# An FFN's right operands summed by adding DMAs, and its last chunk by seven products

## The chip, the core and the metric

The kernel runs on one core of a Trainium2 chip. The metric is the device time of one execution in microseconds (us); before the change it is 1135.33 us, the median of 3 runs (1135.29 to 1135.79). The five engines are TensorE (PE, with its weight loads PEld), VectorE (DVE), ScalarE (ACT), GpSimd (POOL) and SyncE (SP), which issues the DMAs of the kernel before.

## The reference

Two layers over x of 512 tokens by 1024 columns, in float32. Layer 0 mixes tokens by latent attention, layer 1 by an mLSTM; each is followed by the same feed-forward network, the part that matters here, with 4096 hidden columns:

```python
def sqrelu_mlp(h, w1, w2):
    return jnp.square(jax.nn.relu(h @ w1)) @ w2

def reference(x, norm_mix, norm_ffn, ...):
    for i in range(DEPTH):
        hn = rms_norm(x, norm_mix[i])
        ...
        x = x + y.astype(x.dtype)
        x = x + sqrelu_mlp(rms_norm(x, norm_ffn[i]), ffn_w1[i], ffn_w2[i]).astype(x.dtype)
    return x
```

## The kernel before

The program has four stages in a row: latent attention, FFN 0 (about 244 to 581 us of the span), mLSTM, FFN 1 (about 791 us to the end, 1134). Every product of two float32 matrices is made of three matmuls in fp32r: each operand is split into a high part (a cast, on ACT) and a low part (operand less high part, on DVE). For a weight the parts are called wh and wl (`split_w`, lines 155 to 170), for the hidden activations hh and hl.

One FFN is cut along its 4096 hidden columns into 8 chunks c (`NC`). In a chunk the first product takes four units F, each 24 matmuls of 128x512 that give 128 hidden columns for all 512 tokens. `f_post` (lines 755 to 784) runs relu and square on ACT into a tile z; after every second F, GpSimd forms four sums of quarters of z (S1 to S4), and then both halves of z are split into hh and hl, the first 768 columns one unit later, the other 1024 two units later (list `later`).

The second product of chunks 0 to 6 is not a plain product of 2x2 blocks with eight block products but Winograd's form with seven, called P0 to P6 (`PROD`, lines 737 and 738). Each has a left operand (a quarter of hidden activations or a sum), a right operand (a quarter b11 to b22 of the chunk of w2, or one of the sums t1 to t4), and a chain: products of chain a add up in one pair of PSUM banks, those of b and c in another pair, and after each product its state is read by `y_add` (line 827), which adds it, times the norm's factor r2, into the residual x on DVE, once for each token tile. A product has 12 matmuls. Since the next product on a chain writes the same banks, it has to wait for the `y_add` of the one before. The sums t1 to t4 are made by GpSimd out of the loaded quarters (`s_sum`, lines 792 to 801), in tiles tw (6 of them); SP loads the quarters (`s_load`). The last chunk (c = 7) is plain: `l_mm` (line 839), 8 block products of 12 matmuls. In FFN 1 the result is then transposed on TensorE, copied out of PSUM into one of two tiles t (`out`, lines 851 to 864) and stored, 256 KB a time; in FFN 0 it becomes the input of the mLSTM (`Norm.half`).

TensorE, DVE, ACT and GpSimd run in program order here (class `InOrder`, lines 72 to 80; all such instructions show as L80 in the profile). The order is the list `units` (lines 867 to 874), with a unit's split two units ahead and w1 loads four units ahead (`ahead`, line 877). Before, a chunk runs as P0 F P1 P2 F P3 P4 F P5 F P6, where the F units belong to the next chunk; chunk 6, with three F units left, as P0 F P1 F P2 P3 F P4 P5 P6. Only SP's queue is ordered by the scheduler.

## Time and profile before

| | before |
|---|---|
| median of 3 runs | 1135.33 us |
| profiled execution | 1136.02 us |
| its span, first to last instruction | 1134.0 us |
| TensorE busy | 1111.6 us, 98% |
| DVE busy | 823.3 us, 73% |
| ACT busy | 557.9 us, 49% |
| GpSimd busy | 451.4 us, 40% |
| mean granted TensorE clock | 0.998 |
| DMA | 104.27 MB, 92 GB/s, 30.1% of 16 engines |

The span is what the trace covers; the profiled execution's own time is 2.0 us longer. TensorE is busy nearly all the time, so the reader looks for the few places where it isn't, and for what it waits there. A tile's name stands without its number: tw is a tile of w2 quarters, wr one of w1, x the residual, tp and mm PSUM banks.

### The profile page before, as it was taken

Reading aid. Unit: us, or ns where it says so; the run is one execution under the profiler, and the core shown is the slowest. Engines: PE = TensorE matmul, PEld = TensorE weight load, DVE = VectorE, ACT = ScalarE, POOL = GpSimd, SP = SyncE. Lnnn points to the kernel's source line nnn. Section 1 sums busy time; section 2 is a strip of 40 time slices with the busy share of each in tenths; the row PEclk is TensorE's granted clock in tenths of the full one; section 3 lists DMA queues with packets and bytes.
Section 4 is the critical chain, followed back from the end, with each engine's and each line's share of the span. In section 5 each row is a group of like instructions: output and inputs, shape, how many; then the busy total and the mean of one; then the engine's idle time right before and its main releaser. Section 6 shows DMA issues by size and latency. Waiting matters only on the chain.

```text
span 1134.0 us, 15668 instructions
## 1 busy us (share of the span) xinstructions
PE 1111.6 (98%) x5802; PEld 949.0 (84%) x5802; DVE 823.3 (73%) x1286; ACT 557.9 (49%) x985; POOL 451.4 (40%) x454
## 2 busy tenths in 40 slices
PE   7899999999999999999999999999999999999998
PEld 7889988888888888888898898888888888888886
DVE  7689997456798798788756565554578779779863
ACT  4468876336544444534545344332655444444441
POOL 6667785207356347335010011000537437436500
PEclk9999999999999999999999999999999999999999
DMA  6301021433432432343203223232343343333112
GB/s 202 117 25 47 20 76 38 132 98 124 128 99 74 127 112 84 102 123 89 85 21 100 87 59 91 81 90 86 136 113 91 93 130 93 93 112 111 57 56 75
DMA packets 32428, 104.27 MB, mean 92 GB/s; under 512 B 3424, under 2 KB 6752, under 8 KB 32352
## 3 DMA queue, kind: packets, MB, share of 16 engines
q1 hardware_dynamic: 32352, 103.27, 30.1%
q8 instruction: 46, 0.75, 0.3%
q14 instruction: 30, 0.25, 0.1%
HBM read 101.16 MB, written 2.10 MB: 91 GB/s over the span
## 4 chain that ended last, share of the span: by engine, by line
PE 93%; DVE 3%; POOL 2%; ACT 1%; issue 1%; DMA 0%; SPq 0%; ACTq 0%; POOLq 0%
PE mm L80 39%; PE tp L80 38%; PE mm L178 4%; PE mm L177 4%; PE mm L176 4%; PE po L80 3%; PE tp L178 1%; PE tp L177 1%; PE tp L176 1%; DVE wl L80 1%; ACT t L80 1%; DVE x L80 1%; POOL x L80 0%; DMA x<-in_xT 0%; POOL scr L80 0%
## 5 line engine op out<-in xcount | busy, mean ns | idle before, releaser
L80 PE MATMUL mm<-xg,wh 128*128 128x512 f32 (+1 forms) x1088 | 319.1, 377 | 0.0
L80 POOL TENSOR_TENSOR z<-z 128x256 f32<-128x256 f32 x112 | 129.5, 1175 | 320.2 <-ACT z L80 318.0
L80 PEld LDWEIGHTS mm<-xg,wh 128*128 128x128 f32 x1088 | 200.2, 188 | 37.4
L80 DVE TENSOR_TENSOR wl<-tw,wh 128x1024 fp32r<-128x1024 f32 x100 | 174.5, 1745 | 74.9 <-ACT wh L80 74.9
L80 PE MATMUL mm<-xg,wl 128*128 128x512 f32 (+1 forms) x544 | 206.3, 379 | 0.0
L80 POOL TENSOR_TENSOR tw<-tw,tw 128x1024 f32<-128x1024 f32 x56 | 159.8, 2862 | 34.6 <-issue 29.2
L80 DVE SCALAR_TENSOR_TENSOR x<-tp,r,x 128x512 f32<-128x512 f32 (+1 forms) x215 | 149.8, 733 | 14.2 <-PE tp L80 14.1
L80 PE MATMUL tp<-wh,hl 128*128 128x512 f32 x408 | 159.0, 390 | 0.9 <-DVE hl L80 0.9
L80 DVE TENSOR_TENSOR wl<-wr,wh 128x1024 fp32r<-128x1024 f32 (+1 forms) x72 | 119.6, 1661 | 55.4 <-ACT wh L80 55.4
L80 PE MATMUL tp<-wh,hh 128*128 128x512 f32 x408 | 159.1, 390 | 0.0
L80 PE MATMUL tp<-wl,hh 128*128 128x512 f32 x408 | 158.7, 389 | 0.0
L80 ACT ACTIVATE t<-mm 128x512 f32<-128x512 f32 (+3 forms) x97 | 54.3, 560 | 204.1 <-PE mm L80 195.0
L80 PEld LDWEIGHTS mm<-xg,wl 128*128 128x128 f32 x544 | 102.3, 188 | 22.9 <-DVE wl L80 4.5
L80 ACT CAST wh<-tw 128x1024 fp32r<-128x1024 f32 x100 | 104.7, 1047 | 34.1 <-PE tp L80 26.2
L80 ACT CAST wh<-wr 128x1024 fp32r<-128x1024 f32 (+1 forms) x74 | 78.9, 1067 | 32.1 <-PE tp L80 27.7
L166 DVE TENSOR_TENSOR wl<-wr,wh 128x1024 fp32r<-128x1024 f32 (+2 forms) x43 | 51.2, 1194 | 55.8 <-ACT wh L162 55.6
L80 PEld LDWEIGHTS tp<-wh,hl 128*128 128x128 f32 x408 | 76.6, 188 | 17.7 <-DVE hl L80 1.7
L80 PEld LDWEIGHTS tp<-wh,hh 128*128 128x128 f32 x408 | 76.6, 188 | 16.5 <-ACT zw L80 0.8
L80 PEld LDWEIGHTS tp<-wl,hh 128*128 128x128 f32 x408 | 76.6, 188 | 15.8
L80 ACT CAST hh<-z 128x1024 fp32r<-128x1024 f32 (+1 forms) x60 | 56.9, 949 | 53.0 <-POOL z L80 53.0
L80 DVE TENSOR_TENSOR hl<-z,hh 128x1024 fp32r<-128x1024 f32 (+1 forms) x60 | 80.7, 1345 | 0.0
L162 ACT CAST wh<-wr 128x1024 fp32r<-128x1024 f32 (+2 forms) x43 | 42.8, 995 | 66.7 <-PE mm L177 31.6
(281 smaller groups left out, 2063.7 us busy)
## 6 DMA issues: line engine op xcount, KB each, us to landing
wr<-in_w SPq DMA_DIRECT2D x64, 512.0 KB, 3.6
tw<-in_w SPq DMA_DIRECT2D x64, 512.0 KB, 3.6
wr<-in_w_qkv SPq DMA_DIRECT2D x8, 640.0 KB, 4.1
wr<-in_w_oa SPq DMA_DIRECT2D x8, 512.0 KB, 3.7
wr<-in_w_mo SPq DMA_DIRECT2D x8, 512.0 KB, 3.5
wr<-in_w_ob SPq DMA_DIRECT2D x8, 512.0 KB, 3.6
wr<-in_w_v SPq DMA_DIRECT2D x6, 512.0 KB, 3.9
wr<-in_w_z SPq DMA_DIRECT2D x8, 336.0 KB, 4.9
```

The costliest lines, as they stand in the source:

```text
L80: return lambda *args, **kw: tc.keep_in_program_order(f(*args, **kw)) if self.on else f(*args, **kw)
L162: act.copy(hi[:, :n], raw[:, :n])
L166: dve.tensor_sub(lo[:, :n], raw[:, :n], hi[:, :n].bitcast(F32))
L176: pe.matmul(out, lhsT=lh, rhs=rh, start=start, stop=False)
L177: pe.matmul(out, lhsT=lh, rhs=rl, start=False, stop=False)
L178: pe.matmul(out, lhsT=ll, rhs=rh, start=False, stop=stop)
```

## The change

GpSimd no longer subtracts tw tiles. The left operands' signs are turned so that every right sum is a sum without minus (up to the sign, which goes into r2: `r2[:, 1]` is its negative), and each is made by a DMA on GpSimd's queue that reads a quarter of w2 and adds it to what lies in the tile (`accum_op=add`): t1 = b12 + b11, then in the same tile t2 = t1 + b22 and t4 = t2 + b21, each after the split that reads the sum before; t3 = b22 + b12. A chunk has four such DMAs beside four loads on SP. The high part of the negated sums is made by ACT with scale -1, the low part by a scalar_tensor_tensor on DVE.

The order of the products changes (S2 t2 and S4 b22, and S3 t3 and A12 b21, change places), and the units of chunks 0 to 5 run as P0 P1 F P2 P3 F P4 P5 F P6 F; chunk 6 stays P0 F P1 F P2 P3 F P4 P5 P6.

The last chunk is made by the seven products too: P0, P1, P4, P2, P3, then P5 and P6 cut by token tile with outputs between. Its sums t1 to t3 stand in halves of two z tiles, begun by three loads of b12 and adding DMAs during chunk 6; t4 is one tensor_add on GpSimd. In numbers: 24 matmuls fewer (12 in each FFN), 56 subtractions on GpSimd replaced by 64 adding DMAs and 2 additions.

The diff's core:

```diff
-        PROD = ((A11, "b11", "a", (0, 0)), (S1, "t1", "b", (1, 1)), (S2, "t2", "a", (0, 1)), (S4, "b22", "b", (0, 1)),
-                (S3, "t3", "a", (1, 1)), (A12, "b21", "c", (0, 0)), (A22, "t4", "a", (1, 0)))
+        PROD = ((A11, "b11", "a", (0, 0)), (S1, "t1", "b", (1, 1)), (S4, "b22", "b", (0, 1)), (S2, "t2", "a", (0, 1)),
+                (A12, "b21", "c", (0, 0)), (S3, "t3", "a", (1, 1)), (A22, "t4", "a", (1, 0)))
+        PLACE = {"b11": "b11", "b12": "b12", "b22": "b22", "b21": "b21", "t1": "b12", "t2": "b12", "t4": "b12", "t3": "b22"}
+        ADD = {"t1": "b11", "t2": "b22", "t4": "b21", "t3": "b12"}
...
+                else:
+                    iact.activation(hi[:, b], z[:, b], AF.Copy, scale=-1.0)
+                    idve.scalar_tensor_tensor(lo[:, b], z[:, b], -1.0, hi[:, b].bitcast(F32), op0=mult, op1=sub)
...
+            later.append([s_now[0] + 1, lambda: split(slice(0, 3), 1)])
+            later.append([s_now[0] + (2 if i > 3 else 1), lambda: split(slice(3, 7), -1)])
...
+        def l_load():
+            C = NC - 1
+            for n in ("t1", "t2"), ("t3", "t4"):
+                z = fp.tile([P, 2, D], F32, tag="z", bufs=3, name=nm("z"))
+                for i in range(2):
+                    tw[C, n[i]] = z[:, i]
+                    if n[i] != "t4":
+                        nc.sync.dma_start(z[:, i], a["w2"][layer, C, QUARTER.index("b12")])
+        def l_sum(*todo):
+            for n, b in todo:
+                ipool.dma_start(tw[NC - 1, n], a["w2"][layer, NC - 1, QUARTER.index(b)], accum_op=add)
         def s_sum(c, n):
-            b = lambda n: tw[c, n]
-            if n == "t1":
-                tw[c, n] = fp.tile([P, D], F32, tag="tw", bufs=6, name=nm("tw"))
-                ipool.tensor_sub(b("t1"), b("b12"), b("b11"))
-            else:
-                x, y, to = {"t2": ("b22", "t1", "b11"), "t3": ("b22", "b12", "b12"), "t4": ("b21", "t2", "t1")}[n]
-                ipool.tensor_sub(b(to), b(x), b(y))
+            ipool.dma_start(tw[c, PLACE[n]], a["w2"][layer, c, QUARTER.index(ADD[n])], accum_op=add)
         def s_split(c, n):
...
+            if n in (1, 2, 3) and c < NC - 1:
+                s_sum(c, ("t2", "t3", "t4")[n - 1])
...
-        for c in range(NC - 1):
-            for k in range(7):
+        for c in range(NC):
+            for k in range(7) if c < NC - 1 else (0, 1, 4, 2, 3):
                 units.append(("P", c, k))
-                if k in ((0, 2, 4, 5) if c < NC - 2 else (0, 1, 3)):
+                if n < 4 * NC and k in ((1, 3, 5, 6) if c < NC - 2 else (0, 1, 3)):
...
+        C = NC - 1
+        s_mm(C, 5, (0,))()
+        half(0, (0,))
+        s_mm(C, 5, (1,))()
+        half(0, (2, 4, 6))
+        s_mm(C, 6, (0,))()
+        half(1, (4, 6))
         if last:
-            out(4, (3,))
+            post = s_mm(C, 6, (1,))
+            out(0, (2,))
+            post()
...
+            out(0, (3,))
```

How the rows of an order read: operation, the tile written, the tiles read, the shape, and what it waits for.

DVE, the end of chunk 6 in FFN 1, before. The rows begin at the split of P6's right operand (wl from tw); hl is the hidden activations' low part, x from tp a `y_add`, tp_1849 and tp_1850 the banks of chain a, tp_1859 and tp_1860 those of P5.

```order
L80 TENSOR_TENSOR wl_1882_10343<-tw_1840_10085,wh_1881_10342 128x1024 [waits PE_49,Activation_49]
L80 TENSOR_TENSOR hl_1880_10329<-z_1867_10252,hh_1879_10328 128x1024 [waits Activation_49]
L80 SCALAR_TENSOR_TENSOR x_689_3187<-tp_1849_10144,r2_1506_8032,x_689_3187 128x512 [waits PE_49]
L80 SCALAR_TENSOR_TENSOR x_691_3191<-tp_1850_10145,r2_1506_8032,x_691_3191 128x512 [waits PE_49]
L80 TENSOR_TENSOR wl_1886_10355<-tw_1871_10274,wh_1885_10354 128x1024 [waits DMAHW2_49,Activation_49]
L80 SCALAR_TENSOR_TENSOR x_684_3177<-tp_1859_10199,r2_1506_8032,x_684_3177 128x512 [waits PE_49]
L80 SCALAR_TENSOR_TENSOR x_686_3181<-tp_1860_10200,r2_1506_8032,x_686_3181 128x512 [waits PE_49]
L80 TENSOR_TENSOR zw_1887_10372<-tw_1883_10350,zw_1887_10372 128x1024 [waits DMAHW4_49,Activation_49]
L80 SCALAR_TENSOR_TENSOR x_688_3185<-tp_1849_10144,r2_1506_8032,x_688_3185 128x512 [waits PE_49]
L80 SCALAR_TENSOR_TENSOR x_690_3189<-tp_1850_10145,r2_1506_8032,x_690_3189 128x512 [waits PE_49]
```

The same place now; tp_1841 and tp_1842 are chain a, on which both P5 and P6 run, and tp_1851 and tp_1852 are the banks of P4.

```order
L80 TENSOR_TENSOR wl_1875_10372<-tw_1802_9899,wh_1874_10371 128x1024 [waits DMASW3_49,PE_49,Activation_49]
L80 TENSOR_TENSOR hl_1873_10354<-z_1859_10271,hh_1872_10353 128x768 [waits Activation_49]
L80 SCALAR_TENSOR_TENSOR x_684_3177<-tp_1851_10214,r2_1505_8051,x_684_3177 128x512 [waits PE_49]
L80 SCALAR_TENSOR_TENSOR x_686_3181<-tp_1852_10215,r2_1505_8051,x_686_3181 128x512 [waits PE_49]
L80 TENSOR_TENSOR wl_1879_10396<-tw_1865_10298,wh_1878_10395 128x1024 [waits DMAHW2_49,Activation_49]
L80 SCALAR_TENSOR_TENSOR hl_1873_10354<-z_1859_10271,hh_1872_10353 128x1024 [waits Activation_49]
L80 SCALAR_TENSOR_TENSOR x_689_3187<-tp_1841_10155,r2_1505_8051,x_689_3187 128x512 [waits PE_49]
L80 SCALAR_TENSOR_TENSOR x_691_3191<-tp_1842_10156,r2_1505_8051,x_691_3191 128x512 [waits PE_49]
L80 TENSOR_TENSOR wl_1881_10417<-z_1861_10275,wh_1880_10416 128x1024 [waits DMASW4_49,Activation_49]
L80 SCALAR_TENSOR_TENSOR x_688_3185<-tp_1841_10155,r2_1505_8051,x_688_3185 128x512 [waits PE_49]
L80 SCALAR_TENSOR_TENSOR x_690_3189<-tp_1842_10156,r2_1505_8051,x_690_3189 128x512 [waits PE_49]
```

Between the y_adds of P4 and those of P5, DVE now has wl of the next chunk's P0 and the low part of the last 1024 columns; the rows of hl with 768 columns and with the negated 1024 are new here, since the last chunk now needs the sums too.

TensorE, the same place now: the last matmuls of P5 and the first of P6.

```order
L80 MATMUL tp_1842_10156<-wh_1869_10346,hl_1808_9935 128x512
L80 MATMUL tp_1842_10156<-wh_1869_10346,hh_1830_10090 128x512
L80 MATMUL tp_1842_10156<-wl_1870_10347,hh_1830_10090 128x512
L80 MATMUL tp_1842_10156<-wh_1869_10346,hl_1831_10091 128x512
L80 MATMUL tp_1841_10155<-wh_1874_10371,hh_1807_9934 128x512 [waits DVE_49,Activation_49]
L80 MATMUL tp_1841_10155<-wl_1875_10372,hh_1807_9934 128x512
L80 MATMUL tp_1841_10155<-wh_1874_10371,hl_1808_9935 128x512
L80 MATMUL tp_1841_10155<-wh_1874_10371,hh_1830_10090 128x512
```

And before: the last matmuls of P5, on the banks of chain c, and the first of P6, on those of chain a.

```order
L80 MATMUL tp_1860_10200<-wh_1876_10321,hl_1809_9897 128x512
L80 MATMUL tp_1860_10200<-wh_1876_10321,hh_1835_10057 128x512
L80 MATMUL tp_1860_10200<-wl_1877_10322,hh_1835_10057 128x512
L80 MATMUL tp_1860_10200<-wh_1876_10321,hl_1836_10058 128x512
L80 MATMUL tp_1849_10144<-wh_1881_10342,hh_1808_9896 128x512 [waits DVE_49,Activation_49]
L80 MATMUL tp_1849_10144<-wl_1882_10343,hh_1808_9896 128x512
L80 MATMUL tp_1849_10144<-wh_1881_10342,hl_1809_9897 128x512
L80 MATMUL tp_1849_10144<-wh_1881_10342,hh_1835_10057 128x512
```

P5 and P6 stand on one pair of banks now; before they had a pair each.

DVE, the end of FFN 1, now: t are the two tiles out of which the results are stored, mm a PSUM bank with transposes, x from tp the y_adds of P5 (the first two) and P6 of the last chunk.

```order
L80 SCALAR_TENSOR_TENSOR x_689_3187<-tp_1882_10422,r2_1505_8051,x_689_3187 128x512 [waits PE_49]
L80 SCALAR_TENSOR_TENSOR x_691_3191<-tp_1883_10423,r2_1505_8051,x_691_3191 128x512 [waits PE_49]
L80 COPY t_1899_10544<-mm_1898_10539 128x512 [waits PE_49]
L80 COPY t_1903_10560<-mm_1902_10555 128x512 [waits DMAHW3_49,DVE_49,PE_49]
L80 SCALAR_TENSOR_TENSOR x_688_3185<-tp_1882_10422,r2_1505_8051,x_688_3185 128x512 [waits PE_49]
L80 COPY t_1907_10583<-mm_1906_10578 128x512 [waits DMAHW5_49,DVE_49,PE_49]
L80 SCALAR_TENSOR_TENSOR x_690_3189<-tp_1883_10423,r2_1505_8051,x_690_3189 128x512 [waits PE_49]
```

And before, where x from tp are the y_adds of the last four pieces of the plain chunk.

```order
L80 SCALAR_TENSOR_TENSOR x_688_3185<-tp_1894_10451,r2_1506_8032,x_688_3185 128x512 [waits DVE_49,PE_49]
L80 COPY t_1899_10479<-mm_1898_10474 128x512 [waits PE_49]
L80 SCALAR_TENSOR_TENSOR x_690_3189<-tp_1895_10452,r2_1506_8032,x_690_3189 128x512 [waits DVE_49,PE_49]
L80 COPY t_1903_10508<-mm_1902_10503 128x512 [waits DMAHW7_49,DVE_49,PE_49]
L80 SCALAR_TENSOR_TENSOR x_689_3187<-tp_1904_10511,r2_1506_8032,x_689_3187 128x512 [waits PE_49]
L80 COPY t_1909_10539<-mm_1908_10534 128x512 [waits DMAHW1_49,DVE_49,PE_49]
L80 SCALAR_TENSOR_TENSOR x_691_3191<-tp_1905_10512,r2_1506_8032,x_691_3191 128x512 [waits PE_49]
```

Before, the second and third copy here wait for a DMA, and one piece's y_add stands between any two copies; now the first two copies stand together behind P5's y_adds, and both y_adds of P6 stand behind a copy that waits for a DMA.

## Rows read from the trace of the kernel before

**Rows 1.** The page, first part: busy time, share of the span and instructions of each engine.

```profile
PE 1111.6 (98%) x5802; PEld 949.0 (84%) x5802; DVE 823.3 (73%) x1286; ACT 557.9 (49%) x985; POOL 451.4 (40%) x454
```

**Rows 2.** The chain that ended last: start us, us, engine, tile, line, instructions.

```profile
318.52 5.73 PE mm L80 x24
324.25 5.44 PE tp L80 x24
...
1070.43 5.71 PE mm L80 x24
```

**Rows 3.** Waits of the weight loads: us in total, times, longest us.

```profile
PEld mm L80 <- DVE wl L80: 4.5, 12, 0.4
```

**Rows 4.** Timeline of TensorE at the start of FFN 0; brackets: idle before, releaser.

```profile
275.84 0.50 PE L80 MATMUL tp<-wh,hl 128*128 128x512 f32 x1 [0.43 <-DVE hl L80]
```

**Rows 5.** The page, costliest groups: busy us, mean ns, idle before.

```profile
L80 POOL TENSOR_TENSOR tw<-tw,tw 128x1024 f32<-128x1024 f32 x56 | 159.8, 2862 | 34.6 <-issue 29.2
```

**Rows 6.** Timeline of all engines after a unit F in FFN 0.

```profile
345.85 0.39 PE L80 MATMUL tp<-wh,hh 128*128 128x512 f32 x1
...
347.38 4.65 POOL L80 TENSOR_TENSOR z<-z 128x256 f32<-128x256 f32 x4 [17.03 <-ACT z L80]
...
348.28 1.74 DVE L80 TENSOR_TENSOR wl<-tw,wh 128x1024 fp32r<-128x1024 f32 x1 [4.75 <-ACT wh L80]
...
349.94 1.49 DVE L80 TENSOR_TENSOR hl<-z,hh 128x768 fp32r<-128x768 f32 x1
...
351.36 1.40 DVE L80 SCALAR_TENSOR_TENSOR x<-tp,r,x 128x512 f32<-128x512 f32 x2
...
352.07 1.05 ACT L80 CAST hh<-z 128x1024 fp32r<-128x1024 f32 x1 [2.14 <-POOL z L80]
...
352.68 2.80 DVE L80 TENSOR_TENSOR wl<-tw,wh 128x1024 fp32r<-128x1024 f32 x1
```

**Rows 7.** Timeline after the last unit F of FFN 1, chunk 6.

```profile
1097.45 1.23 DVE L80 TENSOR_TENSOR wl<-tw,wh 128x1024 fp32r<-128x1024 f32 x1 [4.75 <-ACT wh L80]
...
1098.59 1.22 DVE L80 TENSOR_TENSOR hl<-z,hh 128x1024 fp32r<-128x1024 f32 x1
...
1099.73 1.40 DVE L80 SCALAR_TENSOR_TENSOR x<-tp,r,x 128x512 f32<-128x512 f32 x2
...
1100.23 0.39 PE L80 MATMUL tp<-wh,hl 128*128 128x512 f32 x1
...
1100.62 0.47 PE L80 MATMUL tp<-wh,hh 128*128 128x512 f32 x1
```

**Rows 8.** Lines 790 (w2 loads) and 863 (outputs): issue ns, then landing us.

```profile
L790 SPq DMA_DIRECT2D tw<-in_w x64: 327/328/886, 242.4 to 1090.3; - x64
...
DMA to landing us min/median/max: 3.4/3.6/6.7
...
L863 SPq DMA_DIRECT2D out_yT<-t x8: 372/372/405, 1118.3 to 1130.8; - x8
...
DMA to landing us min/median/max: 2.2/2.2/4.2
```

**Rows 9.** Timeline of TensorE and ScalarE, last chunk of FFN 1 to the end.

```profile
1103.46 0.39 PE L80 MATMUL tp<-wh,hh 128*128 128x512 f32 x1
...
1128.35 0.59 ACT L80 COPY t<-mm 128x512 f32<-128x512 f32 x1 [2.32 <-DMA out_yT<-t]
1130.16 0.59 ACT L80 COPY t<-mm 128x512 f32<-128x512 f32 x1 [1.23 <-PE mm L80]
```

**Rows 10.** Timeline of TensorE at the start, and its longest pause later.

```profile
6.12 0.68 PE L80 MATMUL tp<-wh,xgh 128*128 128x416 f32 x1 [6.12 <-DVE xgh L210]
...
9.97 0.41 PE L80 MATMUL mm<-wh,xgh 128*128 128x256 f32 x1
10.19 0.41 PE L80 MATMUL mm<-wl,xgh 128*128 128x256 f32 x1
...
165.21 0.66 PE L80 MATMUL tp<-cst,x 128*128 128x128 f32 x4 [1.68 <-DVE sm L80]
```

More of the change, by code (lines that the diff above doesn't have):

```diff
@@ L814, in s_mm @@
+        def s_mm(c, n, ts=(0, 1)):
+            lhs, _, chain, (th, f) = PROD[n]
+            wh, wl = ws["P", c, n]
+            new = n in (0, 1, 4)
+            if ts[0] == 0:
+                if n < 2:
+                    bank[chain] = [ps_tp(), ps_tp()]
+                elif n == 4:
+                    bank["c"] = bank["b"] if c < NC - 1 else [ps_mm(), ps_mm()]
+            banks = list(bank[chain])
+            for t in ts:
+                ps = banks[t]
                 for p in range(2):
@@ L822, in post @@
             def post():
-                for t in range(2):
-                    y_add(2 * th + t, f, bank["b" if chain == "c" else chain][t])
+                for t in ts:
+                    y_add(2 * th + t, f, banks[t])
             return post
         def y_add(t, f, ps):
-            idve.scalar_tensor_tensor(xs[t, f], ps, r2[:, t:t + 1], xs[t, f], op0=mult, op1=add)
-        def l_split(n, roomy):
-            to = None
-            if roomy:
-                z = fp.tile([P, 2, D], F32R, tag="z", bufs=3, name=nm("zw"))
-                to = z[:, 0], z[:, 1]
-            ws["L", n] = split_w(tw[NC - 1, n], D, iact, idve, to=to)
-        def l_mm(th, f, t, part=slice(0, 12)):
-            ps = bank["L", f][t]
-            todo = []
-            for h in range(2):
-                wh, wl = ws["L", f"b{h + 1}{f + 1}"]
-                for p in range(2):
-                    lh, ll = (x[:, ((A11, A12), (3, A22))[th][h], t * P:(t + 1) * P] for x in hs[NC - 1, p])
-                    rh, rl = (x[:, p * 512:(p + 1) * 512] for x in (wh, wl))
-                    todo += [(lh, rh), (lh, rl), (ll, rh)]
-            for n in range(12)[part]:
-                ipe.matmul(ps, lhsT=todo[n][0], rhs=todo[n][1], start=n == 0, stop=n == 11)
+            idve.scalar_tensor_tensor(xs[t, f], ps, r2[:, f, t:t + 1], xs[t, f], op0=mult, op1=add)
         def out(m, ts):
@@ L907, in ffn @@
         f_post(ps[1], 1)
-        s_load(0, ("b11", "b12"))
+        s_load(0, ("b11", "b12", "b22", "b21"))
         s_sum(0, "t1")
-        s_load(0, ("b21", "b22"))
-        s_sum(0, "t3")
-        for s_ in range(2, len(units)):
+        for s_ in range(2, len(units) - 2):
             u = units[s_]
```

112 lines of the change are left out of this document (49 added, 63 removed).

## The prediction

> **What bounds the kernel now.** I read the page's first part and then the chain that ended last: TensorE is busy 1111.6 of 1134.0 us [rows 1], and in both FFNs the chain runs through its units almost without a hole: 5.44 us for the 24 matmuls of a w1 unit F or of two products P, so a matmul of 512 columns costs 0.2267 us and a product 2.72. Twelve F units took 5.69 to 5.73 instead, the first at 318.52, the last at 1070.43 [rows 2]; the waits of the weight loads name the cause, 12 times DVE's subtraction wl, at most 0.4 us each [rows 3]. So two things pay here: matmuls less, and a stall of TensorE less or more. All other engines matter only where TensorE waits for them, and since DVE keeps program order, the question at each place is what stands ahead in DVE's queue.
>
> **Matmuls.** The last chunk has 7 x 12 = 84 instead of 96, in each FFN 12 x 0.2267 = 2.72 us less. In FFN 0 I take all of it: **-2.72**. In FFN 1 the tail decides, below.
>
> **Sums off GpSimd.** The 56 tw subtractions took 2.86 us each [rows 5] and slow DVE beside them: wl took 1.23 us where GpSimd was idle [rows 7], 1.74 beside the four sums z and 2.80 beside a tw sum [rows 6]. With the tw sums gone the second cost goes, 1.6 us or so out of DVE's queue per overlap, against stalls of 0.27 on average. I take all twelve to vanish: 1.63 us in FFN 0 and 1.60 in FFN 1 (the excess over 5.44, summed over the twelve pieces), **-3.23**. At the start of each FFN TensorE waited 0.43 us for hl [rows 4]; the second half of that split now comes a unit earlier and no tw sum stands beside it, but the sums z stay, so I count **-0.7** for both together, between 0 and -0.9. These are the gains that don't depend on anything late.
>
> **The adding DMAs.** Per chunk four, on GpSimd's queue, each ordered behind the plain load of its tile or behind DVE's read of the last sum in it. Nothing in the trace issues from that queue or adds, so the price is bounded: from below by the plain load of the same 512 KB, 3.6 us in the middle [rows 8]; from above by twice the longest, 2 x 6.7 = 13.4, since such a DMA has to read the tile as well as write it. I take 6, nearer to twice a typical one (7.2) than to the far end. The shortest cover is that of t2: from the split of t1 to that of t2 TensorE does P0, P1 and F = 10.88 us, less a cast (1.05) and a subtraction (1.23) that must end first [rows 6, 7] = 8.6 us. So at 6 us they cost nothing, and the transfers themselves (30% of the DMA engines are in use now) have room. If that cover is gone, ACT stops at the cast, and behind it in ACT's order stand relu and square of the F unit, behind those GpSimd's sums.
>
> **The new wait: P6 after P5 in chunk 6.** Chunk 6 has only three F units, and none stands after P4 there. Before, P5 ran on the other pair of PSUM banks; now S3 t3 is P5, and P5 and P6 (A22 t4) both add into chain a, so P6 can't begin before DVE's y_add has read what P5 left. Ahead of that y_add DVE has a queue. I count from X, the end of the F unit before P4, by the stretch of before where an F with sums z ended the same way (X = 345.85, when the next product began; GpSimd's sums begin at X+1.53 and end at X+6.18; DVE's rows are those there [rows 6]):
> wl of P6 starts at X+2.43 (behind relu, square and cast) and takes 1.74 beside the sums; the first 768 columns of hl start at X+4.09; the two y_adds of P4 at X+5.51; wl of the next chunk's first product at X+6.83, and without a tw sum beside it it takes 1.13 from start to start (1097.45 to 1098.59 [rows 7]) instead of 2.80, to X+7.96; the rest of hl, whose hh ACT cast from X+6.22 to X+7.27, another 1.13, to X+9.09. Only then y_add of P5, 0.73, and TensorE follows 0.16 later, as before P6 began at 1100.62 after a y_add that ended at 1099.73 + 0.73 [rows 7]: X+9.98. TensorE wants P6 at X+5.44. Stall **4.5 us in each FFN, +9.0**. If GpSimd and DVE did not slow each other at all, wl, hl, wl and hl would take 1.13, 0.85 (three quarters of it), 1.13 and 1.13 from start to start and the stall would be 3.4; a longer wait for GpSimd, which now has three DMAs to issue just ahead of these sums, makes it longer, to perhaps 6. Before, that same wait for the y_add cost 0.16 us (1100.46 to 1100.62 [rows 7]) in each FFN, which the 4.5 contain: **-0.3**. In chunks 0 to 5 an F unit, 5.44 us, stands between P5 and P6 and covers the queue. In the last chunk the products (S2 t2) and (S3 t3) are neighbours on chain a; there only one wl is ahead, TensorE loses about 0.5: **+0.5** for FFN 0 (FFN 1's is in the tail).
>
> **The tail of FFN 1.** Before, the last chunk's first matmul started at 1103.46 and the last output copy began at 1130.16 [rows 9], so 27.3 us to its end. Now the five products up to (S2 t2) take 13.6 us, to E. All eight outputs come after E, on two tiles t: each needs a copy (0.6 to 0.7) and the landing of the transfer (2.2 [rows 8]) before its tile is free; ACT's copy at 1128.35 had waited 2.32 for one after the copy of 0.59 before it, a cycle of 2.9 [rows 9]. The second tile has outputs m=2, 6, (1,6) and the last: its first copy follows the second half of P5 and its y_adds, at about E+0.3+2.72+0.4 (transposes)+1.2 = E+4.6; three cycles of 2.9 to 3.0 later, at E+13.3 to E+13.7, the last copy, 0.6 more to its end, E+14.3 as I take it: 13.6 + 14.3 = 27.9. Both P6 y_adds stand in DVE's queue behind copies that wait for such a transfer, so nothing overtakes this. The 2.72 us of matmuls are therefore not seen at the end: **+0.6** instead of -2.72. From below: without waits for transfers the tail would be about 3 us shorter than before; from above: two first transfers at the longest, 4.2 [rows 8], add 2.
>
> **Sum.** -2.72 - 3.23 - 0.7 - 0.3 + 9.0 + 0.5 + 0.6 = +3.15. The profiled execution took 1136.02 us around its span of 1134.0; against it 1139.2, against the median of the runs, 1135.33, 1138.5. I say 1138.4.
>
> **Two rules beside the rows.** DVE and GpSimd are seen to hold each other up on SBUF (1.23 against 2.80 [rows 6, 7]); I take an adding DMA to be free of this, 6 us, and if its issue waits for one such subtraction it lands at 8.8, still about the cover of 8.6. The Trainium skill, "SBUF — State Buffer", section "Who interferes with whom", speaks against the change here: a DMA that seems stalled by a DVE operation was issued from GpSimd, which was starved of port time for writing descriptors. No run here has such a DMA; if the rule bites, it is the rival on late DMAs.
> TensorE ran on at the same pace after the longest pause in the trace (1.68 us [rows 10]). The Trainium skill, "TensorE: Matmul & The Clock Gate", Part 1, has the clock fall back to the lower level when TensorE has been idle; a pause as long as that of this forecast is in no row, and what the fall would cost is the rival on the clock.
>
> **Rivals.**
> *Faster: the queue at P6 is short.* Place: y_add of P5 in chunk 6. If the sums z and the splits around F end sooner than in the stretch of [rows 6], or the compiled waits let P6 start, the +9.0 shrinks; at no stall the time is 1129.4. It decides under half of the 9.0: the rest of the sum is -5.85, so the change is faster by over 0.2% only when each stall is below 1.8 us. Against it: even the undisturbed queue gives 3.4. For it: the order of these instructions is known, their times under the new load are not. Time 1129 to 1133. Chance 0.17.
> *The tail keeps its gain.* If two tiles t are no limit (earlier copies than I set), FFN 1 saves its 2.7 and the time is 1135. Against it speak two waits of ACT for out_yT already before, the later one 2.32 [rows 9]. Chance 0.12.
> *Late adding DMAs.* From 8.6 us to landing ACT stands still at each t2, and from some 10 TensorE does; each us beyond costs up to 1 us in 14 chunks' worth of products, at 11 us +14: 1152, at 13.4 about 1180. An issue held by DVE for 2.8 on top of 7.2 reaches 10. Chance 0.10.
> *The clock.* The first matmul is at 6.12, and at 9.97 and 10.19 128x256 matmuls were still 0.22 apart, twice 0.2267 / 2 [rows 10]: the lower level, 1.2 GHz, against 2.4 in the FFNs. The longest pause in mid-run, 1.68 us before 165.21 [rows 10], left the pace as it was. A pause of 4.5 is not in the trace; if the pace fell after it for as long as at the start (over 4 us, I take 5), each FFN loses up to 2.5: 1140 to 1143. Chance 0.11.
> *The change doesn't relieve DVE* (the DMAs' descriptors keep GpSimd at SBUF as the sums did): the twelve stalls stay, 1141.6. Chance 0.05.
>
> **How the numbers follow.** The forecast, 1136 to 1141 with its bounds, has the remaining 0.45. A measurement of this kernel can tell about 0.2%, 2.3 us: faster is under 1133.1, slower over 1137.6. Of the forecast's 0.45 I put 0.16 below 1137.6 (stalls near 3.4, tail a little better) and 0.29 above. Faster: 0.13 of the first rival = 0.13. Same: 0.16 + 0.12 + 0.04 = 0.32. Slower: 0.29 + 0.10 + 0.11 + 0.05 = 0.55. The range leaves out the deeper half of the first rival and the late DMAs: 1131 to 1144. The forecast's own range is 1136 to 1141.
>
> **What would show it.** Right: F units of 5.44 throughout; at the end of chunk 6 in each FFN a hole of some 4.5 us in TensorE's row, its releaser DVE's x (y_add), with wl, hl and STT hl back to back before it; outputs every 3 us at the end with copies waiting for out_yT. Wrong: P6 following P5 at once, casts wh waiting for adding DMAs, matmuls 0.45 apart after the hole, or the last output less than 25 us after the last chunk's first matmul.

## The result: 7.1 us slower, and the profile after

The changed kernel takes 1142.44 us (median of 4 runs, 1141.97 to 1144.81) against 1135.31 us of the kernel before (4 runs, 1134.79 to 1135.79): a ratio of 1.0063, with an interval of 1.0051 to 1.0075. It is slower, by 0.6%. The forecast was 1138.4 us, in a range of 1131 to 1144: the direction and the range hold, but 4 us are missing, and the time lies above the 1136 to 1141 that the prediction gave for its likeliest case. It lies where the rival on the clock stood (1140 to 1143).

The profiled execution of the changed kernel took 1142.03 us around a span of 1140.3 us, 6.3 us more span than before. The page's first part (busy us, share of the span, instructions of each engine) answers to [rows 1]:

```profile
PE 1105.4 (97%) x5778; PEld 946.8 (83%) x5778; DVE 773.2 (68%) x1310; ACT 566.9 (50%) x995; POOL 367.1 (32%) x480
```

TensorE is busy 6.2 us less, DVE 50 us and GpSimd 84 us less, and the kernel is slower: no engine's total tells that. The chain that ended last (start us, us, engine, tile, instructions) shows where to look. It answers to [rows 2]:

```profile
1069.89 5.44 PE mm L80 x24
...
1088.93 5.46 PE mm L80 x24
1098.31 1.49 DVE hl L80
1104.20 10.04 PE tp L80 x36
```

The F units that took 5.69 to 5.73 now take 5.44 to 5.46; only the first one behind P1 in each FFN takes 5.51 and 5.50. The chain has no stalled unit left up to the last F of chunk 6. What GpSimd's sums had cost is seen at the wl that the F unit at 318.52 waited for, in the trace before:

```profile
315.46 3.41 DVE L80 TENSOR_TENSOR wl<-wr,wh 128x1024 fp32r<-128x1024 f32 x1
```

It stood beside two tw sums of GpSimd (314.53 to 321.14); in the trace after, the split at the same place starts at 316.47, with nothing on GpSimd beside it, and takes 1.22.

At the end of chunk 6 the row of units breaks. There the chain leaves TensorE for DVE, and comes back 9.8 us after the end of that F. The same place in FFN 0, TensorE's timeline (start us, us, what; in brackets idle time before and its releaser), with X = 545.24, the end of the last F:

```profile
545.24 0.39 PE L80 MATMUL tp<-wh,hh 128*128 128x512 f32 x1
...
550.45 0.39 PE L80 MATMUL tp<-wh,hl 128*128 128x512 f32 x1
555.22 0.76 PE L80 MATMUL tp<-wh,hh 128*128 128x512 f32 x1 [4.38 <-DVE x L80]
555.78 0.63 PE L80 MATMUL tp<-wl,hh 128*128 128x512 f32 x1
556.21 0.63 PE L80 MATMUL tp<-wh,hl 128*128 128x512 f32 x1
...
558.67 0.40 PE L80 MATMUL tp<-wh,hl 128*128 128x512 f32 x1
```

Two things are to be seen. P6 begins at 555.22 = X+9.98 instead of X+5.44, after 4.38 us without a matmul, released by a `y_add` (DVE x). And then its matmuls follow each other after 0.43 us, not 0.2267, until about 558.7: P6 takes 4.37 us where 2.72 is usual. The table by stretch (us, busy us of PE, PEld, DVE, ACT and POOL, then PEclk, DMA share and GB/s) says why, for that place in both FFNs:

```profile
555.00:559.00 4.00, 3.78 (x10) 3.05 (x11) 2.62 (x4) 0.00 (x0) 2.07 (x1) 0.57 0.29 57
1104.00:1108.50 4.50, 4.30 (x12) 3.42 (x13) 2.59 (x4) 0.00 (x0) 2.36 (x1) 0.62 0.24 46
```

The granted clock is 0.57 and 0.62 of full speed: after the pause TensorE ran mostly at its lower level, 1.2 GHz instead of 2.4.

What TensorE waited for, in DVE's row of the same stretch (answers to [rows 6, 7]), with ACT and GpSimd from the same window:

```profile
547.67 1.74 DVE L80 TENSOR_TENSOR wl<-tw,wh 128x1024 fp32r<-128x1024 f32 x1 [4.75 <-ACT wh L80]
549.34 1.49 DVE L80 TENSOR_TENSOR hl<-z,hh 128x768 fp32r<-128x768 f32 x1
550.75 1.40 DVE L80 SCALAR_TENSOR_TENSOR x<-tp,r,x 128x512 f32<-128x512 f32 x2
552.07 1.21 DVE L80 TENSOR_TENSOR wl<-tw,wh 128x1024 fp32r<-128x1024 f32 x1
553.20 1.21 DVE L80 SCALAR_TENSOR_TENSOR hl<-z,hh 128x1024 fp32r<-128x1024 f32 x1
554.34 1.39 DVE L80 SCALAR_TENSOR_TENSOR x<-tp,r,x 128x512 f32<-128x512 f32 x2
```

```profile
546.78 4.62 POOL L80 TENSOR_TENSOR z<-z 128x256 f32<-128x256 f32 x4 [2.42 <-ACT z L80]
551.36 0.87 POOL L80 DMA_DIRECT2D z<-in_w  x1
```

DVE works without a gap from X+2.43 until both `y_add`s of P5 are done at X+10.5, in the predicted order; the first instruction stands beside GpSimd's sums and takes 1.74 instead of 1.21. The `y_add`s of P5 start at 554.34 = X+9.10.

The waits (us in total, times, longest us) name the same in their second line, and then the waits of the tail:

```profile
ACT wh L80 <- DMA tw<-in_w: 18.8, 10, 2.5
...
PE tp L80 <- DVE x L80: 9.8, 3, 4.4
...
ACT t L80 <- DMA out_yT<-t: 9.1, 4, 2.4
...
DVE t L80 <- DMA out_yT<-t: 4.2, 2, 2.4
...
PEld mm L80 <- DVE wl L80: 0.4, 2, 0.2
```

The last line is that of [rows 3]: 12 waits and 4.5 us before, 2 and 0.4 now. The first line is new: ten of ACT's casts wait for a tw tile.

The DMA issues (KB each, median us to landing) have three kinds that are new or slower; before, a tw load took 3.6 [rows 8]:

```profile
tw<-in_w SPq DMA_DIRECT2D x62, 512.0 KB, 4.2
tw<-in_w POOLq DMA_DIRECT2D x56, 512.0 KB, 5.7
...
z<-in_w POOLq DMA_DIRECT2D x8, 512.0 KB, 8.4
```

Last the tail of FFN 1, ACT's copies of the outputs, which answer to [rows 9]:

```profile
1124.51 0.59 ACT L80 COPY t<-mm 128x512 f32<-128x512 f32 x1 [6.78 <-PE mm L80]
1127.42 0.59 ACT L80 COPY t<-mm 128x512 f32<-128x512 f32 x1 [2.33 <-DMA out_yT<-t]
1130.36 0.59 ACT L80 COPY t<-mm 128x512 f32<-128x512 f32 x1 [2.35 <-DMA out_yT<-t]
...
1135.91 0.58 ACT L80 COPY t<-mm 128x512 f32<-128x512 f32 x1 [1.95 <-DMA out_yT<-t]
```

One copy every 3 us, each waiting for the store out of the same tile: the last one ends 27.87 us after the last chunk's first matmul (1108.62), 27.3 before.

So the two spans compare stretch by stretch (after less before, us; the stretches end at the first matmul of a unit):

| stretch | difference |
|---|---|
| start to FFN 0's first full F | -0.99 |
| FFN 0, first full F to X (end of the last F) | -2.24 |
| FFN 0, X to the last chunk's first matmul | +6.0 |
| FFN 0's last chunk, to the mLSTM's first matmul | -1.2 |
| mLSTM | -0.05 |
| FFN 1, first full F to X | -2.30 |
| FFN 1, X to the last chunk's first matmul | +6.0 |
| FFN 1's last chunk to the end | +1.1 |

Each 6.0 is a stall of 4.54 in the place of 0.16, and 1.65 for the slow matmuls of P6. The first line is no work of the change: the profiled execution of the kernel before had a stretch at half clock in the latent attention, in which it lost 1.4 us against this one of the kernel after, which hadn't:

```profile
66.00:69.00 3.00, 3.00 (x14) 2.81 (x14) 2.56 (x13) 1.43 (x5) 2.32 (x5) 0.50 0.55 201
```

(before; the granted clock is the third number from the end), against 1.00 in the same window after.

### The profile page after: what moved, and what is told of

Read it like the earlier page. It is cut to its first block, busy times and chain, and to the rows that moved or that the text cites. A ratio compares the mean times of both kernels' runs of the same rounds, so it can differ in the third digit from the quotient of the medians.

```text
span 1140.3 us, 15773 instructions
## 1 busy us (share of the span) xinstructions
PE 1105.4 (97%) x5778; PEld 946.8 (83%) x5778; DVE 773.2 (68%) x1310; ACT 566.9 (50%) x995; POOL 367.1 (32%) x480
## 4 chain that ended last, share of the span: by engine, by line
PE 91%; DVE 3%; POOL 2%; issue 1%; DMA 1%; ACT 1%; SPq 0%; DVEq 0%; ACTq 0%; POOLq 0%
PE mm L80 40%; PE tp L80 35%; PE mm L178 4%; PE mm L177 4%; PE mm L176 4%; PE po L80 3%; DVE x L80 1%; PE tp L178 1%; PE tp L177 1%; PE tp L176 1%; DMA out_yT<-t 1%; DVE hl L80 0%; POOL scr L80 0%; POOL x L80 0%; DMA x<-in_xT 0%
## 5 line engine op out<-in xcount | busy, mean ns | idle before, releaser
L80 POOL TENSOR_TENSOR z<-z 128x256 f32<-128x256 f32 x128 | 144.5, 1149 | 353.7 <-ACT z L80 351.2
L80 DVE TENSOR_TENSOR wl<-tw,wh 128x1024 fp32r<-128x1024 f32 x104 | 134.7, 1295 | 89.3 <-ACT wh L80 89.3
L80 PE MATMUL tp<-wh,hh 128*128 128x512 f32 x424 | 166.5, 393 | 8.8 <-DVE x L80 8.8
L80 PE MATMUL tp<-wh,hl 128*128 128x512 f32 x424 | 166.2, 392 | 0.0
L80 PE MATMUL tp<-wl,hh 128*128 128x512 f32 x424 | 166.1, 392 | 0.0
L80 DVE TENSOR_TENSOR wl<-wr,wh 128x1024 fp32r<-128x1024 f32 (+1 forms) x72 | 94.0, 1306 | 101.6 <-ACT wh L80 101.6
L80 DVE SCALAR_TENSOR_TENSOR x<-tp,r,x 128x512 f32<-128x512 f32 (+1 forms) x223 | 155.7, 734 | 6.6 <-PE tp L80 6.5
L80 POOL DMA_DIRECT2D tw<-in_w x56 | 48.9, 873 | 124.1 <-DVE wl L80 124.1
L80 ACT ACTIVATE hh<-z 128x1024 fp32r<-128x1024 f32 x32 | 34.1, 1064 | 68.3 <-POOL z L80 68.3
L80 PE MATMUL mm<-wh,big 128*128 128x256 f32 (+1 forms) x256 | 57.8, 305 | 0.0
```

What stands on the lines that cost most here:

```text
L80: return lambda *args, **kw: tc.keep_in_program_order(f(*args, **kw)) if self.on else f(*args, **kw)
```

## The experiments

Questions were open on four points. What is the hole: the place of two `y_add`s in DVE's queue, which another order could mend, or a lack of DVE time after the last F, which would only move on? Does the lower clock come of the pause? Do the two tiles t set the tail? And what do the adding DMAs cost by themselves? All diffs are against the kernel after unless said otherwise; three dots mark lines left out. Each ratio is to runs of the kernel before that were taken with it (medians 1135.37 to 1135.55 us).

**P5 before P4 in chunk 6**, so that P4, on other banks, stands between P5 and P6.

```diff
-            for k in range(7) if c < NC - 1 else (0, 1, 4, 2, 3):
+            for k in range(7) if c < NC - 2 else (0, 1, 2, 3, 5, 4, 6) if c < NC - 1 else (0, 1, 4, 2, 3):
```

> The changed kernel (1142.4 us) with one thing moved: in chunk 6 of each FFN the products P5 (S3 t3, chain a) and P4 (A12 b21, chain c) change places, so that P5 and P6, which add into the same PSUM banks, are no longer neighbours. Theory A (the neighbours on one chain are the cause): the hole of 4.4 us before P6 shrinks to about 1 us and nothing takes its place, and without a hole the clock stays up: 2 x (3.5 + 1.7) = 10.4 us less, 1132. Theory B (VectorE has more work between the last unit F and the last chunk than TensorE's products there last, in whatever order): the hole is cut in two, some 1 us before P6 and some 3 us before the last chunk's first product, which waits for the y_adds of P6; only the clock's 1.7 us per FFN are saved, 1139.

Measured 1141.35 us (1140.86 to 1141.77), ratio 1.0052 [1.0039, 1.0065]. TensorE's pauses in both FFNs:

```profile
551.37 0.47 PE L80 MATMUL tp<-wh,hh 128*128 128x512 f32 x1 [0.80 <-DVE x L80]
...
573.22 1.19 PE L80 MATMUL tp<-zw,hh 128*128 128x512 f32 x2 [3.97 <-DVE x L80]
```

```profile
1102.05 0.47 PE L80 MATMUL tp<-wh,hh 128*128 128x512 f32 x1 [0.80 <-DVE x L80]
...
1121.39 0.70 PE L80 MATMUL tp<-zw,hh 128*128 128x512 f32 x2 [1.63 <-DVE x L80]
```

The hole of 4.38 at P6 is down to 0.80, but 3.97 us come up in FFN 0's last chunk, at the first matmul of its P5, with the lower clock behind them. The hole moved; it was not mended. In FFN 1 only 1.63 come back at that place, without the lower clock; in FFN 0 splits of the mLSTM's weights stand in DVE's queue there too. The time is 9 us over what was expected if the neighbours alone were the cause, and 2.4 over the other expectation, which had the clock stay up.

**`y_add`s first.** In chunk 6, from P4 on, each product's `y_add`s are put ahead of the hl split and the next wl splits where the waits allow it.

```diff
-            ahead(s_)
+            end = u[0] == "P" and u[1] == NC - 2 and u[2] > 3
...
+            if end:
+                if u[2] == 4:
+                    ahead(s_)
+                    post()
+                else:
+                    post()
+                    later.pop(0)[1]()
+                    ahead(s_)
...
```

> The changed kernel with VectorE's (and ScalarE's) order changed at the end of chunk 6 alone: the y_adds of P4, P5 and P6 each stand ahead of the splits issued in the same unit, and both splits of the hidden activations one unit later, so that only work that a matmul waits for next stands in front. Counted with the durations of the traces from X, the end of the last unit F: P6 at X+6.3 instead of X+9.98, the last chunk at X+9.7 instead of X+12.7 (14.4 with the slow clock): two holes of 0.9 and 0.7 us instead of one of 4.5, no fall of the clock. Theory (the queue in front of the y_adds is the stall): 2 x (2.9 + 1.7) = 9.2 us less, 1133. If the stall were set by something else (a DMA, the banks themselves): 1142.

Measured 1139.36 us (1138.85 to 1139.93), ratio 1.0035 [1.0023, 1.0048]: 3 us better than after, 6 worse than expected. TensorE in FFN 0:

```profile
551.84 0.47 PE L80 MATMUL tp<-wh,hh 128*128 128x512 f32 x1 [0.70 <-DVE x L80]
...
572.92 0.70 PE L80 MATMUL tp<-zw,hh 128*128 128x512 f32 x2 [3.93 <-DVE x L80]
```

and DVE from its first wl after X (545.54) to the last chunk's P5:

```profile
547.97 1.74 DVE L80 TENSOR_TENSOR wl<-tw,wh 128x1024 fp32r<-128x1024 f32 x1 [4.75 <-ACT wh L80]
549.63 2.72 DVE L80 SCALAR_TENSOR_TENSOR x<-tp,r,x 128x512 f32<-128x512 f32 x4
...
560.31 2.11 DVE L80 TENSOR_TENSOR wl<-tw,wh 128x1024 fp32r<-128x1024 f32 x1
...
567.25 1.24 DVE L166 TENSOR_TENSOR wl<-wr,wh 128x1056 fp32r<-128x1056 f32 x1
...
572.04 1.39 DVE L80 SCALAR_TENSOR_TENSOR x<-tp,r,x 128x512 f32<-128x512 f32 x2
```

In the whole row no instruction after the first has idle time before it: DVE is busy from 547.97 to 575.4. So the lack is one of DVE's time. A product gives DVE a split wl (1.13 from start to start, as at 552.07 to 553.20) and two `y_add`s (1.32, as at 550.75 to 552.07), 2.45 us of TensorE's 2.72. As long as F units, which need one wl in 5.44 us, stand between the products, this is easy. After the last F ten products follow in a row, and DVE begins them 2.4 us late, with some 2 us of hl to do, a GpSimd addition beside one wl (2.11), and in FFN 0 three mLSTM splits of 1.17. At 0.27 us a product it can't catch up. The order chooses where TensorE pays for it.

**Filler matmuls.** 18 matmuls into a free bank, whose result nobody reads, stand in TensorE's order between P5 and P6 of chunk 6: the wait stays, the pause goes.

```diff
+                if u[1:] == (NC - 2, 5):
+                    fill, fh = ps_mm(), hs[NC - 2, 0][0]
+                    for n_ in range(18):
+                        ipe.matmul(fill, lhsT=fh[:, 0, 0:P], rhs=fh[:, 0:2, :], start=n_ == 0, stop=n_ == 17)
```

> The changed kernel with 18 more matmuls of 128x512 between P5 and P6 of chunk 6 in each FFN, into a PSUM bank that nobody reads: 4.1 us of work that fits into the hole of 4.4 us. Nothing of the queue changes. If the clock falls because TensorE pauses there: the stall stays (P6 still at X+9.98) but P6's matmuls start 0.227 us apart instead of 0.427, 1.7 us less in each FFN, 1139.0, granted clock 0.998 or more. If the lower clock has another cause: 1142.4, with the half-clock stretch still there.

Measured 1139.07 us (1138.37 to 1139.44), ratio 1.0032 [1.002, 1.0044], 3.4 us less than after.

```profile
550.95 4.24 PE L80 MATMUL mm<-hh 128*128 128x512 f32 x18
555.50 0.47 PE L80 MATMUL tp<-wh,hh 128*128 128x512 f32 x1 [0.30 <-DVE x L80]
555.81 0.39 PE L80 MATMUL tp<-wl,hh 128*128 128x512 f32 x1
556.03 0.40 PE L80 MATMUL tp<-wh,hl 128*128 128x512 f32 x1
```

P6 begins no sooner (9.99 us after the end of the last F), but its matmuls follow at 0.23 instead of 0.43. With other work the same, the lower clock came of TensorE's standing still, and cost 1.7 us in each FFN.

**Outputs in six more tiles.** The first six of the eight outputs are copied into tw tiles, free by then.

```diff
+        outs = [0]
...
-            o = tmp()
+            outs[0] += 1
+            o = fp.tile([P, D], F32, tag="tw", bufs=6, name=nm("o"))[:, 0:512] if outs[0] < 7 else tmp()
```

> The changed kernel with six of the eight output copies of FFN 1 going to free tiles tw instead of the two tiles t, so that no copy waits for an output's DMA. Theory (the tail is set by two tiles, each taken for 2.9 to 3.0 us): the last copy ends at about E+10.8 instead of E+14.3 (E: the end of the product S2 t2 of the last chunk), 3.5 us less, 1138.9. Rival (the tail is set by the chain of y_add, transposes and copies): the same as the changed kernel, 1142.4.

Measured 1141.01 us (1139.17 to 1142.0), ratio 1.0048 [1.0036, 1.0061]. The last copies on ACT:

```profile
1133.66 0.58 ACT L80 COPY t<-mm 128x512 f32<-128x512 f32 x1 [1.67 <-PE mm L80]
1134.79 0.58 ACT L80 COPY t<-mm 128x512 f32<-128x512 f32 x1 [0.54 <-PE mm L80]
```

They wait for TensorE now, not for stores. From the start of P5 of the last chunk to the end of the last copy it is 10.6 us (1124.78 to 1135.37) instead of 14.08 (1122.41 to 1136.49): the 3.5 us are there. The median shows only 1.4 of them, and the span of the profile 0.6 (1139.7). In this profile the lower clock after the pause lasted longer (granted clock 0.58 over the whole of 1104 to 1112): the 36 matmuls from P6 on took 10.77 and 10.64 us in the two FFNs instead of 9.98 and 10.04, 1.4 more. Another 1.0 was lost before FFN 0, with a half-clock stretch at 66 to 70, and the last store ended 0.5 later after its copy. The one run with a mean clock of 0.996 took 1139.17, 2.8 less than after's best.

**The adding DMAs alone.** Right sums by DMA and all that goes with them; the last chunk plain as before; P5 before P4 in chunk 6, so that no neighbours share chain a.

```diff
...
-        for c in range(NC):
-            for k in range(7) if c < NC - 1 else (0, 1, 4, 2, 3):
+        for c in range(NC - 1):
+            for k in range(7) if c < NC - 2 else (0, 1, 2, 3, 5, 4, 6):
...
+        for n, (th, f) in enumerate(((0, 0), (0, 1), (1, 0), (1, 1))):
+            bank["L", f] = [ps_tp(), ps_tp()]
+            for t in range(2):
...
+                    l_mm(th, f, t)
...
```

> The adding DMAs alone: chunks 0 to 6 as in the changed kernel (with P5 and P4 of chunk 6 in exchanged places, so that no neighbours share a chain), the last chunk plain, 8 x 12 matmuls, as in the kernel before. Theory (the sums are a gain of their own, the loss comes from the last chunk's seven products, whose splits and y_adds find VectorE without a unit F beside them): no F unit over 5.45 us, no hole over 1 us at the end of chunk 6, no fall of the clock in the FFNs: 1135.4 - 3.2 - 0.7 = 1131.5. If the adding DMAs cost TensorE something as well: between 1132 and 1135.

Measured 1130.81 us (1129.95 to 1131.61), ratio 0.9959 [0.9947, 0.9972]: 4.6 us faster than before. Its page has TensorE at 98% with all 5802 matmuls, DVE and GpSimd lower than in either kernel:

```profile
PE 1108.7 (98%) x5802; PEld 950.3 (84%) x5802; DVE 750.9 (66%) x1288; ACT 557.8 (49%) x985; POOL 338.0 (30%) x454
```

The trace has no pause of TensorE in either FFN but one of 0.94 at the end. This is the gain that the prediction put at 3.23 + 0.7; the whole loss therefore hangs on the rest of the change, the last chunk by seven products and the neighbours P5 and P6. No run has the new place of the F units without the adding DMAs, or the other way round; that the gain is that of the sums rests on the splits' times, 3.41 beside a tw sum and 1.22 without.

**The neighbours alone.** As the kernel of the adding DMAs alone (the diff is against that), but chunk 6 in the changed kernel's order P4, P5, P6; the loads and splits for the last chunk keep their places in the row.

```diff
-            for k in range(7) if c < NC - 2 else (0, 1, 2, 3, 5, 4, 6):
+            for k in range(7):
...
```

> e6_sums with the products of chunk 6 in the changed kernel's order, P4, P5, P6, so that P5 and P6 are neighbours on chain a again; the last chunk stays plain, so the queue in front of P5's y_adds holds less (no sums z, one split of 1024 columns instead of 768 and 1024). From X, the end of the last unit F: wl 2.43 to 3.57, hl to 4.71, y_adds of P4 to 6.03, wl of the last chunk to 7.16, first y_add of P5 to 7.9, P6 at 8.05 instead of 5.44. Theory (neighbours on one chain cost what stands in VectorE's queue between their y_adds): 2.45 us more per FFN than e6_sums, 1135.7, without a fall of the clock. If the neighbours alone cost nothing and only the last chunk's extra splits did: 1130.8.

Measured 1138.68 us (12 runs, 1134.72 to 1139.59), ratio 1.002 [1.0011, 1.0029]. TensorE at P6:

```profile
553.75 0.76 PE L80 MATMUL tp<-wh,hh 128*128 128x512 f32 x1 [2.45 <-DVE x L80]
...
1102.07 0.47 PE L80 MATMUL tp<-wh,hh 128*128 128x512 f32 x1 [2.45 <-DVE x L80]
```

and the granted clock right after each (third number from the end):

```profile
554.00:558.00 4.00, 4.00 (x12) 3.15 (x13) 3.31 (x4) 0.00 (x0) 0.00 (x0) 0.60 0.18 17
...
1102.00:1106.00 4.00, 3.93 (x12) 3.16 (x13) 2.46 (x3) 0.00 (x0) 0.00 (x0) 0.66 0.00 0
```

So of a stall of 4.54 us, 2.6 (a pause of 2.45 and the pipeline around it) come of the neighbours alone, and the other 2 of the last chunk's sums: with a plain last chunk DVE has one hl less in the queue, and no GpSimd sums beside the first wl (1.23 there instead of 1.74). Two runs of the twelve had a mean clock of 0.999 or 1.0 and took 1134.7, 1 us under the 1135.7 expected without a fall of the clock; eight with 0.994 to 0.996 took 1137.4 to 1139.6. The expectation had the pause as too short for the clock to fall; that was wrong.

**Work moved past the last F.** The last chunk by seven products as in after, the F units of chunk 6 after P1, P3 and P5 instead of P0, P1 and P3 (so the last one stands between P5 and P6), the last chunk in the order P0, P4, P1, P2, P3, P5, P6, `y_add`s ahead of splits there, and the six output tiles.

```diff
...
-            for k in range(7) if c < NC - 1 else (0, 1, 4, 2, 3):
+            for k in range(7) if c < NC - 1 else (0, 4, 1, 2, 3):
                 units.append(("P", c, k))
-                if n < 4 * NC and k in ((1, 3, 5, 6) if c < NC - 2 else (0, 1, 3)):
+                if n < 4 * NC and k in ((1, 3, 5, 6) if c < NC - 2 else (1, 3, 5)):
...
```

> The whole change with its end put in another order: chunk 6 runs as P0 P1 F P2 P3 F P4 P5 F P6, so that only eight products instead of ten follow the last unit F and P5 and P6 are parted by 5.44 us; the last chunk as P0, P4, P1, P2, P3, P5, P6, so that the sums of hidden activations are needed 5.4 us later; VectorE's order there by what a matmul waits for next; six outputs in free tiles. Counted with the traces' durations VectorE is still behind by 1 to 2 us in FFN 1 and by some 2.5 more in FFN 0, where three splits of the mLSTM's weights (1.17 each) stand in its queue, against 6.4 and 6.0 before P5 of the last chunk in the changed kernel; no pause over 2 us, no fall of the clock; the tail 3.5 shorter: 1142.4 - 9.7 + 2.5 - 3.5 = 1131.7, under both kernels. If VectorE's shortage doesn't shrink with the last F unit's place: 1136.

Measured 1134.77 us (11 runs, 1133.53 to 1136.42), ratio 0.9992 [0.9983, 1.0001]: as fast as before, 3 us over what was expected. FFN 1 has pauses of 0.27 to 0.50 only; FFN 0 has these two:

```profile
562.50 0.50 PE L80 MATMUL tp<-wh,hl 128*128 128x512 f32 x1 [1.51 <-DVE hl L80]
573.21 0.70 PE L80 MATMUL tp<-zw,hh 128*128 128x512 f32 x2 [2.75 <-DVE x L80]
```

The lower clock follows the second (0.68 in 573 to 577), not the first (1.00 in 563 to 572). In FFN 1, where no next stage lays its splits into DVE's queue, this order leaves little; in FFN 0 it doesn't pay.

**Each FFN its own.** FFN 0 as in the kernel of the adding DMAs alone, FFN 1 as in the last one (its function stands beside the other as `ffn7`).

```diff
...
     with stage("ffnp1", 2) as pool:
-        ffn(pool, 1, True)
+        ffn7(pool, 1, True)
```

> FFN 0 as in e6_sums (adding DMAs, last chunk plain), FFN 1 as in e7_late (seven products in the last chunk, late last unit F, outputs in free tiles). From the profiles of these two: FFN 0 took 334.6 us from its first matmul to the mLSTM's in e6_sums and 338.8 in e7_late; FFN 1 from its first matmul to the end 340.6 in e6_sums and 340.4 in e7_late. So 0.2 us under e6_sums, 1130.6: the 2.72 us of matmuls of FFN 1 would be gained and given back by VectorE's shortage (1.0) and the longer end. If the seven products pay where VectorE has room: 1128 to 1129.

Measured 1130.29 us (5 runs, 1129.65 to 1130.40), ratio 0.9952 [0.994, 0.9964]. The fastest kernel of the study, 5.3 us under before; but only 0.5 under the adding DMAs alone, well inside the two intervals. The 2.72 us of matmuls that seven products save in FFN 1 are mostly spent again. Four pauses of 0.27 to 0.50, 1.5 in all against one of 0.94, take 0.5 of it; that all outputs now come after the fifth product is the likely place of the rest, and was not measured by itself.

**Plain DMAs in place of the adding ones** in chunks 0 to 6: GpSimd's queue still issues them with the same waits, but they overwrite the tile: the kernel leaves the sums out.

```diff
-            ipool.dma_start(tw[c, PLACE[n]], a["w2"][layer, c, QUARTER.index(ADD[n])], accum_op=add)
+            ipool.dma_start(tw[c, PLACE[n]], a["w2"][layer, c, QUARTER.index(ADD[n])])
```

> The changed kernel with plain DMAs in place of the adding ones in chunks 0 to 6, from the same queue at the same places (the right operands are then quarters, not sums). If adding costs nothing that TensorE sees: the same as the changed kernel, 1142 to 1143, with landings shorter than the 5.7 us of the adding ones, some 4. If the adding DMAs hold TensorE: up to 3 us less.

Measured 1144.35 us (4 runs, 1143.40 to 1144.87), ratio 1.0078 [1.0064, 1.0092]. The landing falls from 5.7 to 3.9:

```profile
tw<-in_w POOLq DMA_DIRECT2D x56, 512.0 KB, 3.9
```

and the pauses at P6 are the same 4.38 in both FFNs. No cast waits for a tw tile here, so the ten waits of ACT in the kernel after are the adding's. TensorE doesn't see them: from FFN 0's first matmuls (244.79 here, 243.69 in after) to P6 it is 311.47 us against 311.53. The adding itself costs 1.8 us of landing and nothing at TensorE.

This kernel is no faster but 1.9 us slower than after. In its trace the lower clock after the pauses lasts about twice as long (0.59 over the whole of 556 to 563 and 0.57 over 1104 to 1112), as in the kernel with six more output tiles; the 36 matmuls from P6 on take 11.00 and 10.79 us, 1.8 more than in after, and 1.1 of the profile's span was lost before FFN 0. That is no property of this kernel: by their mean clocks the four runs of the kernel after differ in the same way, with 0.995 in those of 1142.03 and 1141.97 us, 0.992 in that of 1142.86 and 0.991 in that of 1144.81. At a mean clock of 0.991 this kernel took 1144.73 and 1144.87.

## Why the prediction was right, and where it was short

- *Twelve F stalls, -3.23, and the start, -0.7*: right, a little low. The F units of the chain take 5.44, the waits for hl at the start are gone, and the stretch from the first F to X is shorter by 2.24 and 2.30, 4.5 together where 3.9 were counted. The adding DMAs alone gave 4.6 over the whole kernel. Some 0.4 us of the 4.5 has no line of its own.
- *Matmuls, -2.72 in FFN 0*: the matmuls are gone, but FFN 0's last chunk is shorter by only 1.2. The pause in it (below) takes 1.1 back; the other 0.4 was not taken apart.
- *Adding DMAs free under a cover of 8.6*: right for TensorE and in the size, 5.7 us where 6 was taken (5.2 to 7.8 in tw tiles), but the cover was mis-sized for ACT. It reached the cast of t2 some 3.8 us after the DMA was issued (318.02 and 314.22), so it stood still at nine of the fourteen, 1.9 to 2.5 us each. "Casts wh waiting for adding DMAs", named as a sign of being wrong, did come; the wait of 18.8 us in all reached no matmul. The rule of the Trainium skill, "SBUF — State Buffer", "Who interferes with whom", that was weighed against this (GpSimd starved of port time for descriptors) did not bite: with 64 such DMAs on that queue, the longest into a tw tile landed after 7.8 us, and the two waits of TensorE for wl that are left are 0.2 each. GpSimd's issue takes 0.87 us of its own time.
- *P6 after P5 in chunk 6, +9.0*: right at the place, X+9.98 worked out, X+9.98 and X+9.99 measured in the two FFNs, and in the predicted order of DVE. This was possible because every instruction of the queue had a row somewhere in the trace before, with and without GpSimd beside it. That it fits to 0.01 us is luck: one row differs from the next of its kind by some hundredths. The kernel with the neighbours alone shows the same sum with fewer terms.
- *What comes after the pause*: this is the step that failed. The prediction took TensorE to run on at full clock, by the 1.68 us pause of [rows 10], and gave the fall of the clock 0.11, at up to 2.5 us per FFN. It came in both FFNs and cost 1.65 each in the profile, 3.4 by the filler matmuls: with it the forecast of 1138.4 would have been 1141.8, against 1142.44. There was evidence for it in the trace before that wasn't read: the half-clock stretch at 66 to 69, after pauses of 1.52 and 0.62 us close together. It was not proof, since in the trace after the clock stayed up at the same place, after 1.47 and 0.62. "No pause that long is in the trace, and after the shorter one the pace stayed" is no reason for a low chance; a pause nearly three times as long as the one cited should have had the fall as its likelier case. The Trainium skill, "TensorE: Matmul & The Clock Gate", Part 1, has the clock fall back when TensorE has been idle; the traces agree, at 4.38 and at 2.45 us. By their mean clock, two runs of the kernel with the 2.45 us pauses had no fall.
- *Neighbours (S2 t2) and (S3 t3) in the last chunk, +0.5*: too low. TensorE paused there for 1.1 in FFN 0, since one split of the mLSTM's weights (1.17 us, at 570.57) had come into DVE's queue ahead of the `y_add`; in FFN 1, without it, P5 followed 0.17 after the product before. The prediction counted the last chunk's queue as if the stage ended there.
- *Tail of FFN 1, +0.6*: right. The last copy ends 27.87 us after the chunk's first matmul where 27.9 was worked out, in cycles of 3.0; the last store landed 0.5 later than before's. That the two tiles t set it is shown by the six more tiles, -3.5 us on that stretch.
- *The rivals*: "faster" asked for stalls below 1.8 us, they were 4.54. "The tail keeps its gain" and "no relief for DVE" did not come. Of "late adding DMAs" only ACT's standing still came, and sooner than at 8.6 us. (By its own rule of 14 us for each one beyond 10, that rival's time at 13.4 us would be 1186, not 1180.)

The sum by stretches: -4.5 (first F to X) + 12.0 (P6, with the clock) - 1.2 + 1.1 and -0.99 that is not the change's, 6.3 us of span. So beside the clock's 3.3 two smaller misses, 1.0 too little saved in FFN 0's last chunk and 0.5 more in the tail, were in part cancelled by a third, 0.6 more gained by F.

One step further than the prediction saw: it treated the wait at P6 as a matter of place, one `y_add` behind the splits ahead of it. With a plain last chunk that is so: P5 before P4 leaves no pause where the other order has 2.45. With seven products in the last chunk it is one of quantity as well, as the two kernels that change the place alone there show. DVE can't keep pace with a row of ten products, and whoever moves its work moves the pause. An estimate from the rows above: the last chunk by seven products asks DVE for 7 x 2.45 = 17.2 us beside 19.0 of TensorE, the plain one, with four splits and eight `y_add`s, for 4 x 1.13 + 8 x 0.66 = 9.8 beside 21.8.

Left open: the 0.4 us of FFN 0's last chunk; where the rest of the 2.72 us goes when FFN 1's last chunk is made by seven products without large pauses; and why in some runs the lower clock lasts twice as long as in others after the same pause.
